# Attention values times weights on TensorE: high and low parts of the values as one stationary operand of 128 columns

## Chip, cores and metric

One NeuronCore of a Trainium2 chip runs the whole program. The metric is the device time of one execution in microseconds (us). The kernel before takes 1706.34 us, the median of 3 runs (1706.33 to 1706.62).

## What is computed

A decoder block on 1024 tokens of 1024 channels, in float32: a root-mean-square norm, one wide input projection, then two mixers side by side (dilated attention and a gated convolution), gates that merge them, an output projection, and a gated feed-forward part. The change concerns the attention. There are three groups of 8 heads of 64 channels, with windows and dilations (128, 1), (512, 4), (2048, 16). A query sees the keys at multiples of the dilation in its window. Cut to what matters:

```python
s = einsum('brnqhd,brnkhd->brnhqk', qb, kb) * Dh ** -0.5 + bias   # scores
s = where(valid, s, -1e30)
lse = logsumexp(s)
p = exp(s - lse)
o = einsum('brnhqk,brnkhd->brnqhd', p, vb)                        # values times weights
...
alpha = softmax(stack(lses), axis=0)       # the groups are merged per head
o = einsum('gbsh,gbshd->bshd', alpha, stack(outs))
```

The kernel keeps nearly float32 accuracy with fp32r matmuls: an operand x is split into a high part `hi`, rounded to fp32r, and a low part `lo = x - hi`, and a product is taken as hi·hi + hi·lo + lo·hi.

## The kernel before

The program is recorded in one fixed order by Python generators (`manual_schedule`), and each engine takes its own instructions in that order. The tile framework adds the semaphores. The order comes from three hand-written devices:

- The main line issues long runs of matmuls (`unit`, `prod`, `v`). After every few of them it calls `tick()`, which moves background generators and steps due at a given tick (`later`), and `beat()`, which moves the attention generator `att` by credit: 0.42 steps per beat while the value projection runs (`RV`), 0.8 afterwards (`RU`).
- `attention` runs 96 steps, one for each pair of heads, group and block of 128 queries (12 passes of 8 blocks), and 5 more to empty its pipeline. Step s issues the scores of block s (`att_s`, L1069 on TensorE, L1072 on VectorE, which adds the bias and takes the row minimum), the exponentials of block s-1 (`att_e`, L1082 on ScalarE), the transposes of the weights of block pair s-4 (`att_t`, L1107 on TensorE; ScalarE copies the high part out of the bank, L1114, VectorE subtracts for the low part, L1115), and the value products of s-5 (`att_p`, L1142). Each `yield` lets matmuls of the main line come between.
- A step k serves one head (k even: first, k odd: second) of a pair of query blocks. So two steps fill one bank, and 48 such pairs of steps make up the stretch.

`att_p` multiplies, for each key block, the values (stationary, keys on the partitions) with the transposed weights (moving, up to 256 queries). The value tile `v` holds, for each key block, 64 columns of high part and then 64 of low part for each head (`value_parts`, L930 on ScalarE, L931 on GpSimd). The three products high·hi, low·hi and high·lo are three matmuls with 66 stationary columns (64 that count and two of what follows) into the same 66 partitions of a bank of tag "o" (2 banks). For the last low part of a tile, which has nothing behind it, GpSimd copies the 64 columns into a small tile `vx` with two zero columns (L935). After the second head VectorE copies the 64 partitions of the bank to the output tile `O`, head by head, 256 queries each, in the order of tokens (L1162). `O` goes to DRAM, and `merge` reads it back for the weighted sum over groups.

The buffers of the stretch: 11 half tiles of 128x512 (tag "c", for scores, hi and lo of the transposed weights, and bias), 42 tiles of 128x1024 (tag "b"), 3 ring tiles (tag "d", among them `O`), and banks g, s, t, o of two each.

Beside the attention run the value projection (L961, L962, with the copy L972 by ScalarE and the sum L983 by GpSimd), then a gate's projection and the convolution's output projection (L318 to L320, weights split in L190/L191), the splits of values' weights (L201/L202) and of the convolution (L1262/L1263), and doubling copies of the queries on GpSimd (L899, L900). SP issues nearly all DMAs, in its own order: loads of queries and keys (L883, L884, L890), bias (L492), values (L911 to L916), convolution (L1333), attention outputs (L1169 out, L1217 back), weights (L177).

Of the kernel before, what the change touches and what calls it, by code (L numbers as in the profile page):

```python
# [10 lines left out]
F32R = mybir.dt.float32r  # L11
AF = mybir.ActivationFunctionType
OP = mybir.AluOpType
# [45 lines left out]
def f(ap):  # L59
    return ap.bitcast(F32)  # L60


class Build:
# [372 lines left out]
    def consts(self):  # L436
        nc = self.nc
        self.ident = self.small.tile([128, 128], F32, name="ident")
        nc.gpsimd.dma_start(self.ident, self.p_ident)
        self.vx = [self.small.tile([128, 66], F32R, name=f"vx{i}") for i in range(4)]  # L440
        for x in self.vx:
            nc.gpsimd.memset(f(x[:, 64:]), 0.0)
        self.mean_col = self.small.tile([128, 1], F32, name="mean_col")
        nc.vector.memset(self.mean_col, 1.0 / D)
        self.eps_rms = self.small.tile([128, 1], F32, name="eps_rms")
        nc.vector.memset(self.eps_rms, RMS_EPS)
        self.eps_ln = self.small.tile([128, 1], F32, name="eps_ln")
        nc.vector.memset(self.eps_ln, LN_EPS)

        warm = self.tiny(1, "warm", 1)  # L450
        nc.scalar.activation(warm, self.eps_ln, AF.Square)
# [473 lines left out]
    def value_parts(self, x, i):  # L925

        v = self.slot(F32R)
        d = v.rearrange("p (t e c) -> p t e c", t=8, e=2)
        y = x[:, i * H:(i + 1) * H].rearrange("p (t c) -> p t c", t=8)
        self.nc.scalar.copy(d[:, :, 0], y)  # L930
        self.nc.gpsimd.tensor_tensor(d[:, :, 1], y, f(d[:, :, 0]), op=OP.subtract)  # L931

        w = self.vx[self.vi % 4]
        self.vi += 1
        self.nc.gpsimd.tensor_copy(w[:, :64], f(d[:, 7, 1]))  # L935
        return v, w

    def v(self, g, hg, now, then):

# [47 lines left out]


    LT, LP = 4, 5
    vi = 0  # L990

    normed = 0

    def attention(self):

        live, s, total = {}, 0, 96
        order = [(g, 2 * hg + i) for hg in range(2) for g in range(3) for i in range(2)]
        nxt, cur, u, x, V = self.stacks(*order.pop(0)), None, 8, None, None
        for i in range(5):
            self.stack_load(nxt)  # L1000
        second, doubled = self.stacks(*order.pop(0)), 0

        def there():
            return nxt[1] // 2 * 3 + nxt[0] < self.vn

        while s < total + self.LP:
            if s < total:
                if x is None and nxt and there():
                    x = self.values(*nxt[:2])
                if u == 8:  # L1010
                    while self.normed < 9 or x is None:
                        if second and second[5] < min(5, self.normed - 6):
                            self.stack_load(second)
                        if cur is None and doubled < min(2, self.normed - 5):
                            self.double(nxt, doubled)
                            doubled += 1
                        if x is None and there():
                            x = self.values(*nxt[:2])
                        yield 0
                    cur, u, nxt, V = nxt, 0, None, []  # L1020
                    self.ending = s == total - 8
                live[s] = a = {}
                self.att_s(a, cur, V, u)
                u += 1

                if u in (4, 5):
                    if len(V) < 2:
                        V.append(self.value_parts(x, u - 4))
                    if u == 5:
                        x = None  # L1030
                if u == 6 and cur[0] == 2:
                    self.other_stats(cur)
                if u in (6, 7) and nxt:
                    self.double(nxt, u - 6)
                if u == 8:
                    cur[2] = cur[3] = V = None
                if u == 1:
                    if second:
                        nxt, second = second, None
                    elif order:  # L1040
                        nxt = self.stacks(*order.pop(0))
                if nxt and nxt[5] < 5:
                    self.stack_load(nxt)
            if 0 <= s - 1 < total:
                self.att_e(live[s - 1])
            yield 0
            if 0 <= s - self.LT < total:
                self.att_t(live, s - self.LT)
                yield 0
            if 0 <= s - self.LP < total:  # L1050
                yield from self.att_p(live, s - self.LP)
            s += 1

    def att_s(self, a, p, V, u):
        nc = self.nc
        g, hp, ops, bt, st = p[:5]
        if g == 0:
            blocks = [u - 1, u] if u else [u]
        elif g == 1:
            blocks = [u - 1, u] if u % 2 else [u]  # L1060
        else:
            blocks = [u]
        n = 128 * len(blocks)
        q, k = slice(u * 128, (u + 1) * 128), slice(blocks[0] * 128, blocks[0] * 128 + n)
        ps = self.bank("s")
        for hh in range(2):
            y, *x = ops[hh]
            for i in range(2):
                nc.tensor.matmul(ps[:, hh * 256:hh * 256 + n], x[i][:, q], y[:, k], start=i == 0, stop=i == 1)  # L1069
        sp = self.half()  # L1070
        for hh in range(2):
            nc.vector.tensor_tensor_reduce(sp[:, hh * 256:hh * 256 + n], ps[:, hh * 256:hh * 256 + n],  # L1072
                                           bt[:, hh * 256 + 256 - n:(hh + 1) * 256], 1.0, 3e38, OP.add, OP.min,
                                           st[:, g, self.place(g, u), hh:hh + 1])
        a.update(g=g, hp=hp, u=u, blocks=blocks, sp=sp, V=V, p=p, n=n)
# [42 lines left out]
    def att_p(self, live, k):  # L1118


        nc = self.nc
        a, b, hh = live[k & ~1], live[k | 1], k & 1
        g, hp, u = a["g"], a["hp"], a["u"]
        if hh == 0:
            a["o"] = self.bank("o")
        ps = a["o"]
        hi, lo = a.pop(("pt", hh))

        if g == 2:
            todo = [(u, 0, 128, 0), (u + 1, 128, 128, 128)]  # L1130
        else:
            n = 256 + 128 * (len(a["blocks"]) > 1)
            todo = [(u, 0, 256, 0)] + [(u - 1, 256, 128, 0)] * (n > 256) + [(u + 1, n, 128, 128)]
        for j, (kb, x, n, q) in enumerate(todo):
            kb = self.place(g, kb)
            v, w = a["V"][kb // 4]
            c = (kb % 4) * 256 + hh * 128
            vh = v[:, c:c + 66]
            vl = v[:, c + 64:c + 130] if c < 896 else w
            o = ps[0:66, hh * 256 + q:hh * 256 + q + n]  # L1140
            for i, (y, z) in enumerate(((vh, hi), (vl, hi), (vh, lo))):
                nc.tensor.matmul(o, y, z[:, x:x + n], start=i == 0 and j == 0, stop=i == 2 and j == len(todo) - 1,  # L1142
                                 skip_group_check=True)
            if j < 2:
                yield 0
        hi = lo = v = w = vh = vl = y = z = None
        if hh == 0:
            return
        if u == 0:
            self.O = self.ring()  # L1150

        O = self.O
        e = (8, 2, 128)[g]
        if g == 0:
            d = O.rearrange("p (c m) -> p m c", c=8)[:, u * 16:u * 16 + 32]
        elif g == 1:
            d = O.rearrange("p (e c m) -> p c m e", e=2, c=4)[:, u // 2]
        else:
            d = O[:, u * 128:u * 128 + 256].rearrange("p (c m) -> p c m", c=2)
        for h in range(2):  # L1160
            x = ps[0:64, h * 256:(h + 1) * 256]
            nc.vector.tensor_copy(d[h * 64:(h + 1) * 64], x.rearrange("p (a e) -> p a e", e=e))  # L1162
        a["o"] = ps = d = x = O = None
        del live[k - 1], live[k]
        if u == 6:

            kept = g == 2 and hp > 1
            if not kept:
                self.later(6, lambda x=self.O: nc.sync.dma_start(self.d_att[g, hp], x))  # L1169
            if g == 2:  # L1170
                self.merges.append(self.bg(self.merge(hp, a["p"][4], self.O if kept else None)))
            self.O = None
# [885 lines left out]
```

## Time and profile before

| | |
|---|---|
| median of 3 runs | 1706.34 us |
| span of the profiled execution, first to last instruction | 1704.7 us |
| TensorE (PE) busy | 1686.8 us, 99% |
| weight loads (PEld) busy | 1417.7 us, 83% |
| VectorE (DVE) busy | 1260.4 us, 74% |
| ScalarE (ACT) busy | 800.6 us, 47% |
| GpSimd (POOL) busy | 499.0 us, 29% |
| granted TensorE clock | 1.000 |
| first and last start of the value products (L1142) | 623.7 and 860.0 us |
| main line from the value projection to L318 | at 792.4 us |
| main line from L318 to the output projection (L1671) | at 969.1 us |

How the profile is read: times are from the start of the span. A row of a group names line, engine, operation, tiles (out<-in, buffer numbers left out), shapes and count; then the time that the group was busy, the mean length of one in ns, and the idle time of its engine just before it with what ended it. A matmul's shape is given as rows*columns of the stationary operand and then the moving operand (128*66 128x256: 66 stationary columns, 256 moving ones). Matmuls overlap each other, so the lengths of single ones add up to more than the time they take, and TensorE's time is read from the distance of their starts. PEld is the loading of stationary operands, which runs beside the matmuls.

### The profile page before, as it was taken

Reading aid. Unit: us, or ns where it says so; the run is one execution under the profiler, and the core shown is the slowest. Engines: PE = TensorE matmul, PEld = TensorE weight load, DVE = VectorE, ACT = ScalarE, POOL = GpSimd, SP = SyncE. Lnnn points to the kernel's source line nnn. Section 1 sums busy time; section 2 is a strip of 40 time slices with the busy share of each in tenths; the row PEclk is TensorE's granted clock in tenths of the full one; section 3 lists DMA queues with packets and bytes.
Section 4 is the critical chain, followed back from the end, with each engine's and each line's share of the span. In section 5 each row is a group of like instructions: output and inputs, shape, how many; then the busy total and the mean of one; then the engine's idle time right before and its main releaser. Section 6 shows DMA issues by size and latency. Waiting matters only on the chain.

```text
span 1704.7 us, 23850 instructions
## 1 busy us (share of the span) xinstructions
PE 1686.8 (99%) x8374; PEld 1417.7 (83%) x8374; DVE 1260.4 (74%) x2216; ACT 800.6 (47%) x1574; POOL 499.0 (29%) x397
## 2 busy tenths in 40 slices
PE   8999999999999999999999999999999999999998
PEld 7788888888888889999888888888888888888886
DVE  6789988888999767777885845675565556677686
ACT  6344344434444576777712436633333333354463
POOL 0017777887886254655300310000000000000000
PEclk9999999999999999999999999999999999999999
DMA  4252433455567887778998722133223322494234
GB/s 166 104 185 87 149 124 130 152 196 177 173 167 176 269 266 211 222 218 224 311 290 294 254 74 88 68 111 112 93 93 112 111 93 93 155 376 137 102 133 155
DMA packets 162357, 283.39 MB, mean 166 GB/s; under 512 B 47249, under 2 KB 78732, under 8 KB 162236
## 3 DMA queue, kind: packets, MB, share of 16 engines
q1 hardware_dynamic: 161516, 281.18, 51.2%
q8 instruction: 66, 1.08, 0.3%
q0 software_dynamic: 432, 0.42, 0.1%
q14 instruction: 55, 0.45, 0.1%
q10 hardware_dynamic: 288, 0.27, 0.0%
HBM read 191.10 MB, written 95.42 MB: 168 GB/s over the span
## 4 chain that ended last, share of the span: by engine, by line
PE 94%; DMA 2%; ACT 1%; POOL 1%; issue 1%; DVE 1%; SPq 0%; DVEq 0%; ACTq 0%; POOLq 0%
PE p L334 15%; PE p L335 15%; PE p L336 15%; PE p L1942 12%; PE p L961 5%; PE p L1671 5%; PE p L318 5%; PE p L320 5%; PE p L319 5%; PE p L1142 3%; PE p L962 2%; PE p L1069 2%; PE p L569 2%; PE p L1107 2%; DMA b<-dk 1%
## 5 line engine op out<-in xcount | busy, mean ns | idle before, releaser
L334 PE MATMUL p<-b,b 128*128 128x512 f32 x1204 | 469.3, 390 | 0.5 <-ACT c L353 0.3
L335 PE MATMUL p<-b,b 128*128 128x512 f32 x1204 | 469.0, 389 | 0.0
L336 PE MATMUL p<-b,b 128*128 128x512 f32 x1204 | 468.9, 389 | 0.0
L334 PEld LDWEIGHTS p<-b,b 128*128 128x128 f32 x1204 | 226.1, 188 | 48.5 <-DVE c L853 1.0
L336 PEld LDWEIGHTS p<-b,b 128*128 128x128 f32 x1204 | 226.0, 188 | 47.0
L335 PEld LDWEIGHTS p<-b,b 128*128 128x128 f32 x1204 | 226.1, 188 | 46.8
L1942 PE MATMUL p<-b,b 128*128 128x512 f32 x924 | 209.6, 389 | 0.0
L1942 PEld LDWEIGHTS p<-b,b 128*128 128x128 f32 x924 | 173.5, 188 | 35.9
L699 DVE SCALAR_TENSOR_TENSOR p<-b,par,p 128x511 f32<-128x511 f32 (+14 forms) x232 | 163.3, 738 | 0.0
L318 PE MATMUL p<-b,b 128*128 128x512 f32 x368 | 147.3, 400 | 0.0
L961 PE MATMUL p<-b,b 128*128 128x512 f32 x384 | 145.0, 410 | 0.0
L320 PE MATMUL p<-b,b 128*128 128x512 f32 x368 | 143.8, 391 | 0.0
L319 PE MATMUL p<-b,b 128*128 128x512 f32 x368 | 143.6, 390 | 0.0
L208 ACT CAST b<-d 128x1024 fp32r<-128x1024 f32 x86 | 90.4, 1051 | 105.2 <-POOL d L229 55.1
L209 POOL TENSOR_TENSOR b<-d,b 128x1024 fp32r<-128x1024 f32 x44 | 106.9, 2430 | 79.9 <-ACT b L208 72.5
L209 DVE TENSOR_TENSOR b<-d,b 128x1024 fp32r<-128x1024 f32 x42 | 51.3, 1221 | 101.0 <-ACT b L208 101.0
L1263 DVE TENSOR_TENSOR b<-b,b 128x512 fp32r<-128x512 f32 x133 | 92.0, 696 | 23.2 <-ACT b L1262 21.2
L962 PE MATMUL p<-b,b 128*128 128x256 f32 x384 | 107.7, 281 | 0.0
L1262 ACT CAST b<-b 128x512 fp32r<-128x512 f32 x133 | 82.1, 619 | 47.6 <-PE p L1942 18.4
L1671 PE MATMUL p<-b,b 128*128 128x512 f32 x384 | 89.4, 392 | 0.0
L1082 ACT ACTIVATE c<-c,stat 128x128 f32<-128x128 f32 (+1 forms) x192 | 85.1, 447 | 6.7 <-DVE stat L1072 6.6
L208 ACT CAST b<-b 128x1024 fp32r<-128x1024 f32 x47 | 49.5, 1052 | 78.7 <-POOL b L236 37.2
(234 smaller groups left out, 2910.5 us busy)
## 6 DMA issues: line engine op xcount, KB each, us to landing
b<-w_in SPq DMA_DIRECT2D x30, 512.0 KB, 4.8
dk<-c SPq DMA_DIRECT2D x48, 256.0 KB, 3.0
dq<-c SPq DMA_DIRECT2D x48, 256.0 KB, 3.6
b<-dq SPq DMA_DIRECT2D x48, 256.0 KB, 3.9
b<-dk SPq DMA_DIRECT2D x48, 256.0 KB, 7.1
b<-w_fi SPq DMA_DIRECT2D x24, 512.0 KB, 4.7
d<-w_in SPq DMA_DIRECT2D x23, 512.0 KB, 4.1
dqS<-c SPq DMA_DIRECT2D x44, 256.0 KB, 2.1
```

What stands on the lines that cost most here:

```text
L209: self.wsplit.tensor_tensor(lo, x, f(hi), op=OP.subtract)
L318: nc.tensor.matmul(ps, hi[:, s], a, start=kt == 0, stop=False)
L319: nc.tensor.matmul(ps, hi[:, s], b, start=False, stop=False)
L320: nc.tensor.matmul(ps, lo[:, s], a, start=False, stop=kt == nk - 1)
L334: nc.tensor.matmul(ps, hi[:, s], a, start=first and kt == 0, stop=False, skip_group_check=True)
L335: nc.tensor.matmul(ps, hi[:, s], b, start=False, stop=False, skip_group_check=True)
L336: nc.tensor.matmul(ps, lo[:, s], a, start=False, stop=kt == 3, skip_group_check=True)
L699: nc.vector.scalar_tensor_tensor(A[i][:, j:], src[i][:, :H - j], w[i], A[i][:, j:], op0=OP.mult, op1=OP.add)
L961: nc.tensor.matmul(ps, a, w, start=kt == 0, stop=kt == KT - 1, skip_group_check=True)
L962: nc.tensor.matmul(ps[:, 256:], b, w[:, :256], start=False, stop=kt == KT - 1, skip_group_check=True)
L1671: nc.tensor.matmul(banks[tt][nh], st, wt[:, nh * H:(nh + 1) * H], start=bool(kt == 0 and a), stop=bool(kt == KT - 1 and b))
L1942: nc.tensor.matmul(acc[t], x, y, start=first and e == 0, stop=last and e == 2, skip_group_check=True)
```

## The change

In `att_p`, high and low part of a head's values, which lie side by side in `v`, become one stationary operand of 128 columns. One matmul with the high part of the weights gives high·hi in the bank's partitions 0 to 63 and low·hi in 64 to 127; a second one, with 66 columns as before, adds high·lo to the lower partitions 0 to 65. When both heads are done, ScalarE copies partitions 64 to 127 of the bank into a half tile `low`, and VectorE adds this to partitions 0 to 63 while it writes `O`, in place of its copy. That add is recorded one step later, behind the next block's scores and exponentials (`self.added`). The small tiles `vx`, their four memsets and their 24 copies go.

```diff
@@ value_parts
-        w = self.vx[self.vi % 4]
-        self.vi += 1
-        self.nc.gpsimd.tensor_copy(w[:, :64], f(d[:, 7, 1]))
-        return v, w
+        return v
@@ attention
             if 0 <= s - 1 < total:
                 self.att_e(live[s - 1])
             yield 0
+            if self.added:
+                self.added()
+                self.added = None
             if 0 <= s - self.LT < total:
                 self.att_t(live, s - self.LT)
                 yield 0
             if 0 <= s - self.LP < total:
                 yield from self.att_p(live, s - self.LP)
             s += 1
+        self.added()
+        self.added = None
@@ att_p
-            vh = v[:, c:c + 66]
-            vl = v[:, c + 64:c + 130] if c < 896 else w
-            o = ps[0:66, hh * 256 + q:hh * 256 + q + n]
-            for i, (y, z) in enumerate(((vh, hi), (vl, hi), (vh, lo))):
-                nc.tensor.matmul(o, y, z[:, x:x + n], start=i == 0 and j == 0, stop=i == 2 and j == len(todo) - 1,
-                                 skip_group_check=True)
+            o = ps[:, hh * 256 + q:hh * 256 + q + n]
+            nc.tensor.matmul(o, v[:, c:c + 128], hi[:, x:x + n], start=j == 0, stop=False, skip_group_check=True)
+            nc.tensor.matmul(o[0:66], v[:, c:c + 66], lo[:, x:x + n], start=False, stop=j == len(todo) - 1,
+                             skip_group_check=True)
             if j < 2:
                 yield 0
         if hh == 0:
             return
+        low = self.half()
+        nc.scalar.copy(low[0:64], ps[64:128])
+        del live[k - 1], live[k]
+        self.added = lambda: self.att_o(a, ps, low)
+
+    def att_o(self, a, ps, low):
...
         for h in range(2):
-            x = ps[0:64, h * 256:(h + 1) * 256]
-            nc.vector.tensor_copy(d[h * 64:(h + 1) * 64], x.rearrange("p (a e) -> p a e", e=e))
+            x, y = (z[0:64, h * 256:(h + 1) * 256].rearrange("p (a e) -> p a e", e=e) for z in (ps, low))
+            nc.vector.tensor_tensor(d[h * 64:(h + 1) * 64], x, y, op=OP.add)
```

The rest of what was the end of `att_p` (the ring tile `O`, its order of tokens, the DMA to DRAM, the start of `merge`) moves into `att_o` unchanged and so also comes one step later.

More of the change, by code (lines that the diff above doesn't have):

```diff
@@ L439, in consts @@
         nc.gpsimd.dma_start(self.ident, self.p_ident)
-        self.vx = [self.small.tile([128, 66], F32R, name=f"vx{i}") for i in range(4)]
-        for x in self.vx:
-            nc.gpsimd.memset(f(x[:, 64:]), 0.0)
         self.mean_col = self.small.tile([128, 1], F32, name="mean_col")
@@ L989 @@
     LT, LP = 4, 5
-    vi = 0
+    added = None
     normed = 0
@@ L1135, in att_p @@
             kb = self.place(g, kb)
-            v, w = a["V"][kb // 4]
+            v = a["V"][kb // 4]
             c = (kb % 4) * 256 + hh * 128
-            vh = v[:, c:c + 66]
-            vl = v[:, c + 64:c + 130] if c < 896 else w
-            o = ps[0:66, hh * 256 + q:hh * 256 + q + n]
-            for i, (y, z) in enumerate(((vh, hi), (vl, hi), (vh, lo))):
-                nc.tensor.matmul(o, y, z[:, x:x + n], start=i == 0 and j == 0, stop=i == 2 and j == len(todo) - 1,
-                                 skip_group_check=True)
+            o = ps[:, hh * 256 + q:hh * 256 + q + n]
+            nc.tensor.matmul(o, v[:, c:c + 128], hi[:, x:x + n], start=j == 0, stop=False, skip_group_check=True)
+            nc.tensor.matmul(o[0:66], v[:, c:c + 66], lo[:, x:x + n], start=False, stop=j == len(todo) - 1,
+                             skip_group_check=True)
             if j < 2:
                 yield 0
-        hi = lo = v = w = vh = vl = y = z = None
+        hi = lo = v = None
         if hh == 0:
             return
+        low = self.half()
[3 more added lines that the diff above has]
+    def att_o(self, a, ps, low):
+        nc = self.nc
+        g, hp, u = a["g"], a["hp"], a["u"]
         if u == 0:
@@ L1160, in att_p @@
         for h in range(2):
-            x = ps[0:64, h * 256:(h + 1) * 256]
-            nc.vector.tensor_copy(d[h * 64:(h + 1) * 64], x.rearrange("p (a e) -> p a e", e=e))
-        a["o"] = ps = d = x = O = None
-        del live[k - 1], live[k]
+            x, y = (z[0:64, h * 256:(h + 1) * 256].rearrange("p (a e) -> p a e", e=e) for z in (ps, low))
+            nc.vector.tensor_tensor(d[h * 64:(h + 1) * 64], x, y, op=OP.add)
+        a["o"] = None
         if u == 6:
```

## The prediction

> **What bounds the kernel now.** I read the page first, for the engine that the end hangs on.
>
> ```profile
> span 1704.7 us, 23850 instructions
> PE 1686.8 (99%) x8374; PEld 1417.7 (83%) x8374; DVE 1260.4 (74%) x2216; ACT 800.6 (47%) x1574; POOL 499.0 (29%) x397
> PE 94%; DMA 2%; ACT 1%; POOL 1%; issue 1%; DVE 1%; SPq 0%; DVEq 0%; ACTq 0%; POOLq 0%
> ```
>
> The median, 1706.34 us, is 1.6 us above this span; I work out a change of the span and apply it to the median. TensorE carries 94% of the chain. The change lies in the attention stretch alone, from the first to the last value product (L1142), so I asked for the engines in windows there.
>
> ```profile
> 617.00:660.00 43.00, 41.16 (x328) 38.33 (x328) 30.57 (x102) 32.78 (x102) 22.25 (x30) 1.00 0.87 246
> ...
> 800.00:831.00 31.00, 31.00 (x225) 27.33 (x225) 27.51 (x85) 25.23 (x83) 18.08 (x25) 1.00 0.91 255
> 831.00:861.00 30.00, 28.71 (x208) 24.42 (x207) 25.03 (x85) 17.90 (x63) 4.96 (x6) 1.00 1.05 300
> sum 244.00, PE 240.88 PEld 221.68 DVE 189.09 ACT 176.61 POOL 120.38; mean PE 48.18 PEld 44.34 DVE 37.82 ACT 35.32 POOL 24.08
> ```
>
> After the window and its length the columns are PE, PEld, DVE, ACT, POOL, granted clock (1.00 all along), DMA share and GB/s. TensorE is idle for 3 us of 244. ScalarE is busy 72% (176.6 of 244), VectorE 77%, and the DMA engines 87% in the first of these windows and 91 and 105% in the last two. So a shorter TensorE stream shortens the stretch, until one of these three sets its length.
>
> **What the matmuls save.** The groups of L1142 by shape, then a few of its matmuls in the timeline (start, length from first start to last end, count):
>
> ```profile
> L1142 PE MATMUL p<-c,b 128*66 128x128 f32 x432 | 48.7, 227 | 0.3 <-DVE c L1115 0.3
> L1142 PE MATMUL p<-c,b 128*66 128x256 f32 x188 | 36.5, 298 | 0.8 <-POOL b L931 0.8
> L1142 PE MATMUL p<-c,vx 128*66 128x128 f32 x24 | 5.4, 223 | 0.0
> L1142 PE MATMUL p<-c,vx 128*66 128x256 f32 x4 | 1.1, 280 | 0.0
> ```
>
> Three matmuls make a product, so there are (432+24)/3 = 152 products over 128 queries and (188+4)/3 = 64 over 256. One matmul of each goes: 216. Matmuls overlap, so what one is worth is not its 227 or 298 ns but the distance between starts:
>
> ```profile
> 720.82 0.34 PE L1142 MATMUL p<-c,b 128*66 128x128 f32 x3
> 721.00 0.61 PE L1069 MATMUL p<-b,b 128*128 128x128 f32 x4
> 721.45 0.41 PE L1107 MATMUL p<-ident,c 128*128 128x128 f32 x2
> ...
> 823.45 0.38 PE L1107 MATMUL p<-ident,c 128*128 128x128 f32 x2
> 823.59 0.36 PE L1142 MATMUL p<-c,b 128*66 128x256 f32 x1
> 823.79 0.28 PE L1142 MATMUL p<-c,vx 128*66 128x256 f32 x1
> 823.91 0.28 PE L1142 MATMUL p<-c,b 128*66 128x256 f32 x1
> 824.02 0.40 PE L318 MATMUL p<-b,b 128*128 128x512 f32 x1
> ```
>
> 128 moving columns against 66 stationary ones: three from 720.82 to 721.00, 0.060 us each. 256 columns: 823.79 to 823.91 to 824.02, 0.115 each. Gross saving 152 x 0.060 + 64 x 0.115 = 9.1 + 7.4 = 16.5 us.
>
> The same rows hold the cost. The scores (L1069) also stream 128 columns, but against 128 stationary columns, and take (721.45 - 721.00)/4 = 0.113 each: loading the wider operand is slower than streaming 128 columns. The new first matmul has 128 stationary columns, so wherever it follows a 128-column matmul it starts 0.113 - 0.060 = 0.053 later than now. In the changed program's order 34 new first matmuls stand directly behind the short second one of the product before: 34 x 0.053 = 1.8 us. 59 more stand behind a transpose. There the rows from 823.45 help: two transposes and the product matmul behind them take 823.79 - 823.45 = 0.34, which is 0.115 for the matmul and 0.113 for each transpose. A transpose already takes as long as the wide load, which then hides beside it, and I count nothing; if it hides nothing it is 59 x 0.053 = 3.1. The other 123 stand behind 256 or 512 columns, which take at least 0.115 and cover the load. TensorE's stream gets shorter by 16.5 - 1.8 = **14.7 us**, bounds 11.6 (all 93 places pay) and 16.5 (none does).
>
> A rule of the Trainium skill speaks against the change here: "TensorE: Matmul & The Clock Gate", section "LDWEIGHTS (loading the stationary operand)", gives a load as columns/1.2 ns, 107 for 128 columns and 55 for 66 as an estimate. The trace agrees (0.113 against 0.060). Taken for all 93 places, transposes included, it makes the saving 11.6.
>
> **What is added on ScalarE and VectorE.** 48 copies of 64x512 out of the bank. No row has that shape; the nearest are L972 (128x512 out of a bank, 585) and the first of L1114.
>
> ```profile
> L972 ACT COPY b<-p 128x512 f32<-128x512 f32 x28 | 16.4, 585 | 0.2 <-PE p L962 0.2
> L1114 ACT CAST c<-p 128x384 fp32r<-128x384 f32 (+2 forms) x96 | 44.9, 468 | 53.3 <-PE p L1107 52.6 <-ACT c L1082 0.3
> L1162 DVE COPY d<-p 64x256 f32<-64x256 f32 x96 | 52.6, 548 | 6.8 <-PE p L1142 5.6
> L1115 DVE TENSOR_TENSOR c<-p,c 128x256 fp32r<-128x256 f32 x32 | 13.4, 420 | 6.6 <-ACT c L1114 6.3
> ```
>
> I take 0.585: 48 x 0.585 = 28.1 us; bounds 48 x 0.3 = 14 (if half the partitions halved it) and 28.1; with 14 the 5 us that I give back below would be some 3. ScalarE then has 204.7 us in a stretch of 244 - 14.7 = 229: 89%. Its present idle is mostly the 52.6 us before L1114, waiting for transposes; the copies eat half of that.
>
> VectorE's 96 copies (mean 548) become 96 adds. An add from a bank over 256 elements costs 420 (L1115), inside the copies' own range, so I count 0; at 420 each it would be 12 us less of VectorE, with 0.1 more each 10 us more, 82% busy becoming 87%. POOL loses 24 small casts; it is idle half of the stretch (120.38 of 244 busy) and TensorE's waits for it are under 1 us (0.8 in the second row of L1142), so nothing. Four memsets at the start go, beside loads. SP's order changes in two places, where merges start one step later (four L1333 loads pass L1208, one L1217 passes L1169): I count nothing, since TensorE's one DMA wait in the stretch (the last row of this part) is for another load; were one of these late, it would cost about what that wait does.
>
> **What the new wait holds up.** The copy waits for the last value product of a pair. Queued behind it on ScalarE are two exponentials (L1082) and the next step's L1114; VectorE's L1115 waits for that, and the next value product for L1115. The adds, now a step later, stand behind two L1072, which wait for that step's scores. One pair of now:
>
> ```profile
> 757.45 0.34 PE L1142 MATMUL p<-c,b 128*66 128x128 f32 x3
> ...
> 757.82 1.25 DVE L1162 COPY d<-p 64x256 f32<-64x256 f32 x2 [0.16 <-PE p L1142]
> 757.86 0.50 ACT L1082 ACTIVATE c<-c,stat 128x256 f32<-128x256 f32 x1
> ...
> 758.84 0.59 ACT L1114 CAST c<-p 128x512 fp32r<-128x512 f32 x1 [0.39 <-PE p L1107]
> ...
> 759.80 0.69 DVE L1115 TENSOR_TENSOR c<-p,c 128x512 fp32r<-128x512 f32 x1
> ...
> 761.49 0.59 PE L1142 MATMUL p<-c,b 128*66 128x256 f32 x3
> ```
>
> The product ends at 757.79. The copy would run to 758.41, two exponentials of 0.50 to 759.4, L1114 to 760.0 instead of 759.43: 0.6 late. The rest of the lower part L1115 follows to 760.7 instead of 760.49, or a little more behind the adds. It is needed at the second matmul, 761.6, and 0.3 earlier still when each of 48 pairs is 14.7/48 shorter. So this pair keeps 0.6 us. The cover is gone where the margin is now under 0.9, as it is from 800 to 831, where VectorE has 27.5 of 31 us and ScalarE 25.2 plus 3.5 for six copies, 28.7 of 30. A pair there, in which L1115 ends 0.4 before its product:
>
> ```profile
> 828.00 0.41 DVE L1115 TENSOR_TENSOR c<-p,c 128x256 fp32r<-128x256 f32 x1
> ...
> 828.75 0.53 PE L1142 MATMUL p<-c,b 128*66 128x128 f32 x6
> ```
>
> Estimate: the 12 pairs of 800 to 861 and two or three elsewhere, 0.3 to 0.4 us each (0.9 less some 0.5), 5 us. The end of the stretch leans on DMA already:
>
> ```profile
> 833.04 0.51 PE L1069 MATMUL p<-b,b 128*128 128x128 f32 x2 [1.02 <-DMA b<-dk]
> ```
>
> With the DMA engines full (1.05) that load will not come earlier by what TensorE gains in the same window; I add 1 us. Sum: -14.7 + 5 + 1 = -8.7. **1706.3 - 8.7 = 1697.6 us**, for this case 1694 to 1702.
>
> **Rivals.**
> - *All of it arrives.* Every margin holds, and ScalarE keeps up at 89% as it does at 81% from 800 to 831 now. 1706.3 - 14.7 = 1691.6, at the bound of 16.5 1689.8. Against it: the stretch 800 to 831.
> - *The wide load costs after transposes too* (then 93 x 0.053 = 4.9 instead of 1.8): saving 11.6, with the same 6 given back 1700.7; the change would do less of what it says. For it: the scores pay that price. Against it: the 0.34 from 823.45. [...]
> - *ScalarE and VectorE set the pace and give all of it back.* Light pairs keep their 0.3; pairs with one more piece in the queue (0.585 from an L972, say) lose it again: in the mean 0.3 a pair, the 14.7 is spent. 1703 to 1709, middle 1706. For it: 204.7 of 229 us on an engine that serves in order.
> - *Slower.* Copy, exponentials, L1114, L1115 and value products become one loop. By the rows: 0.6 + 1.0 + 0.6 + 0.7, hand-overs 0.2, products and the work between them 757.79 - 756.08 = 1.7, together 4.8, against a pair of 244/48 = 5.1 now; one more piece of 0.6 to 0.7 inside makes it 5.4 to 5.5. Where more than half of the pairs hold one, the gain of 0.3 in the rest is used up; with 36 of 48 it is 36 x 0.35 - 12 x 0.3 = +9.0: 1715.3. The row for the pair's first product:
>
> ```profile
> 756.08 0.66 PE L1142 MATMUL p<-c,b 128*66 128x256 f32 x4
> ```
>
> **How the numbers follow.** Chances: forecast 0.50, all of it 0.17, wide load 0.08, given back 0.15, slower 0.10. Predicted is the likeliest, 1697.6. Left out of the range are the slower case and the upper half of the given-back one (0.17); it reaches down to the bound of the full gain: 1690 to 1706. A difference under 0.2% (3.4 us) can hardly be told from none here; faster by more than that are the first three, 0.75; within it 0.15; slower 0.10.
>
> **What would show it.** Right: 432 product matmuls, 0.06 apart or 0.115, with 0.113 only at the 34 places; the stretch 7 to 10 us shorter and the rest as it was; ScalarE near 205 us in it, the copy near 0.59; new idle before product matmuls that ends with L1115 or L1114, a few us in all, most after 800. Wrong: the copy well under 0.5, or no new idle (full gain); transposes followed by a product 0.05 later (wide load); an idle before most products (given back or slower); a gain before 861 that is lost after it, in the loads for the merges; any difference outside the stretch.

## The result, and the profile after

The changed kernel takes 1699.02 us (median of 5 runs, 1697.04 to 1700.21) against 1706.62 us of the kernel before beside it: ratio 0.995, 95% interval 0.9938 to 0.9962. It is 7.6 us faster; 8.7 was forecast, and 1697.6 lies 1.4 us below the measured time. The profiled execution took 1700.21 us, with a span of 1698.4.

Line numbers after: L1067 scores, L1070 reduction, L1080 exponentials, L1105 transposes, L1112 high part and L1113 low part of the weights, L1137 the new matmul of 128 stationary columns, L1138 the second one with 66, L1146 ScalarE's copy, L1167 the adds. First the page: span, engines, chain.

```profile
span 1698.4 us, 23450 instructions
PE 1675.6 (99%) x8158; PEld 1404.2 (83%) x8158; DVE 1256.8 (74%) x2216; ACT 826.8 (49%) x1622; POOL 492.6 (29%) x369
PE 90%; DMA 4%; DVE 2%; ACT 1%; issue 1%; POOL 1%; SPq 0%; DVEq 0%; ACTq 0%; POOLq 0%
```

216 matmuls are gone, TensorE's busy time is 11.2 us less, ScalarE's 26.2 more, VectorE's 3.6 less. The stretch itself is read from two rows of the timeline, the first scores and the last value product. First of before, then of after:

```profile
614.31 0.85 PE L1069 MATMUL p<-b,b 128*128 128x128 f32 x6
...
860.00 0.22 PE L1142 MATMUL p<-c,b 128*66 128x128 f32 x1
```

```profile
616.10 0.96 PE L1067 MATMUL p<-b,b 128*128 128x128 f32 x7
...
853.68 0.23 PE L1138 MATMUL p<-c,b 128*66 128x128 f32 x1
```

From start of the first to end of the last it took 245.9 us and takes 237.8: **8.1 us less**. In this profile it begins 1.8 us later; in a second profile of the same changed kernel (E12 below) it begins at 614.93 and lasts 237.7. In these two profiles the stretch repeats within 0.2 us and the time ahead of it does not, so below I compare kernels by their stretch as well as by their medians. The stretch of each kernel is that of one profiled execution, though, and in three of them (E2, E3, E7) it also holds times at a lower clock, told further down. The windows of after, columns as in the prediction:

```profile
...
800.00:831.00 31.00, 27.60 (x181) 23.53 (x181) 27.33 (x88) 26.33 (x83) 10.58 (x13) 1.00 1.03 308
...
sum 237.00, PE 228.34 PEld 207.86 DVE 186.45 ACT 203.13 POOL 114.27; mean PE 45.67 PEld 41.57 DVE 37.29 ACT 40.63 POOL 22.85
```

From 800 to 831 us TensorE was busy all 31 us before; now it stands idle for 3.4. What it waits for, in total, times and longest, from 617 to 870 us, before and then after:

```profile
PE p L1069 <- DVE stat L1072: 2.3, 2, 1.3
PE p L1069 <- DMA b<-dk: 1.0, 1, 1.0
PE p L1142 <- POOL b L931: 0.8, 1, 0.8
PE p L1142 <- DVE c L1115: 0.3, 1, 0.3
```

```profile
PE p L1138 <- DVE c L1113: 4.9, 7, 1.1
PE p L1067 <- DVE stat L1070: 2.0, 2, 1.0
PE p L1137 <- ACT c L1112: 0.8, 1, 0.8
PE p L1067 <- DMA b<-dk: 0.6, 1, 0.6
```

One wait has grown: that of the second matmul for the lower part of the weights, 0.3 to 4.9 us, of which 4.6 fall after 800 us. By passes (8 steps each, one group and two heads), read off the starts of the scores, the first ten passes shrink from 198.47 to 187.32 us and the last two grow from 47.46 to 50.48. So 11.15 us are gained up to 803 us, and 3.02 are lost behind it. One of the stalls, in the order of time:

```profile
816.63 0.58 ACT L1146 COPY c<-p 64x512 f32<-64x512 f32 x1
...
817.89 0.61 ACT L190 CAST b<-b 128x512 fp32r<-128x512 f32 x1
...
818.53 0.88 DVE L191 TENSOR_TENSOR b<-b,b 128x512 fp32r<-128x512 f32 x1 [0.72 <-ACT b L190]
...
819.33 1.23 DVE L1167 TENSOR_TENSOR d<-p,c 64x256 f32<-64x256 f32 x2
...
820.10 0.35 ACT L1112 CAST c<-p 128x256 fp32r<-128x256 f32 x1
...
820.59 0.42 DVE L1113 TENSOR_TENSOR c<-p,c 128x256 fp32r<-128x256 f32 x1
...
821.07 0.28 PE L1138 MATMUL p<-c,b 128*66 128x128 f32 x1 [1.03 <-DVE c L1113]
```

The copy pushes ScalarE's exponentials and its split of another projection's weights (L190) back; VectorE idles 0.72 us for that split, subtracts, adds twice, and only then makes the lower part that TensorE has been waiting for. A first reading is that the adds cost because they stand ahead of L1113; E2 and E3 test it.

### The profile page after: what moved, and what is told of

Read it like the earlier page. It is cut to its first block, busy times and chain, and to the rows that moved or that the text cites. A ratio compares the mean times of both kernels' runs of the same rounds, so it can differ in the third digit from the quotient of the medians.

```text
span 1698.4 us, 23450 instructions
## 1 busy us (share of the span) xinstructions
PE 1675.6 (99%) x8158; PEld 1404.2 (83%) x8158; DVE 1256.8 (74%) x2216; ACT 826.8 (49%) x1622; POOL 492.6 (29%) x369
## 4 chain that ended last, share of the span: by engine, by line
PE 90%; DMA 4%; DVE 2%; ACT 1%; issue 1%; POOL 1%; SPq 0%; DVEq 0%; ACTq 0%; POOLq 0%
PE p L334 15%; PE p L335 15%; PE p L336 15%; PE p L1946 12%; PE p L1675 5%; PE p L954 5%; PE p L318 5%; PE p L319 5%; PE p L320 5%; PE p L955 2%; PE p L1067 2%; PE p L1105 1%; DMA b<-dq 1%; PE p L1138 1%; PE p L1137 1%
## 5 line engine op out<-in xcount | busy, mean ns | idle before, releaser
L1267 DVE TENSOR_TENSOR b<-b,b 128x512 fp32r<-128x512 f32 x133 | 91.9, 695 | 25.0 <-ACT b L1266 23.2
L1266 ACT CAST b<-b 128x512 fp32r<-128x512 f32 x133 | 82.1, 619 | 47.7 <-PE p L1946 18.4
L1080 ACT ACTIVATE c<-c,stat 128x128 f32<-128x128 f32 (+1 forms) x192 | 85.0, 446 | 0.2 <-DVE stat L1070 0.2
```

## Experiments

All 12 runs, each timed in rounds with the kernel before on the same chip. The stretch is that of each one's profile, first score to last value product.

| kernel | median us | before beside it | ratio, 95% interval | stretch us |
|---|---|---|---|---|
| before | | 1706.62 | | 245.9 |
| changed | 1699.02 | 1706.62 | 0.9950 (0.9938 to 0.9962) | 237.8 |
| E1 TensorE's part alone | 1693.31 | 1706.92 | 0.9917 (0.9904 to 0.9930) | 233.9 |
| E2 adds behind L1113 | 1700.71 | 1706.92 | 0.9957 (0.9945 to 0.9968) | 239.0 |
| E3 copy and adds behind | 1700.37 | 1706.92 | 0.9961 (0.9947 to 0.9975) | 243.7 |
| E4 before, wide loads | 1715.50 | 1706.92 | 1.0048 (1.0036 to 1.0061) | 254.5 |
| E5 E1 and ScalarE's copy | 1698.23 | 1707.80 | 0.9946 (0.9934 to 0.9959) | 236.7 |
| E6 E1, VectorE one step later | 1695.52 | 1707.80 | 0.9934 (0.9921 to 0.9947) | 233.2 |
| E7 changed, copy twice | 1710.25 | 1707.80 | 1.0014 (1.0005 to 1.0023) | 249.7 |
| E8 changed, splits on GpSimd | 1697.03 | 1707.80 | 0.9937 (0.9925 to 0.9950) | 235.0 |
| E9 E5, copy from other data | 1696.79 | 1707.27 | 0.9937 (0.9922 to 0.9953) | 235.1 |
| E10 E8, value casts on GpSimd | 1695.84 | 1707.27 | 0.9929 (0.9914 to 0.9944) | 232.4 |
| E11 before, splits on GpSimd | 1708.21 | 1707.27 | 1.0004 (0.9995 to 1.0012) | 246.6 |
| E12 the changed kernel again | 1698.29 | 1707.27 | 0.9945 (0.9930 to 0.9960) | 237.7 |

### E1: TensorE's part alone

```diff
-            if self.added:
-                self.added()
-                self.added = None
...
-        low = self.half()
-        nc.scalar.copy(low[0:64], ps[64:128])
+        low = None
         del live[k - 1], live[k]
-        self.added = lambda: self.att_o(a, ps, low)
+        self.att_o(a, ps, low)
...
-            nc.vector.tensor_tensor(d[h * 64:(h + 1) * 64], x, y, op=OP.add)
+            x = ps[0:64, h * 256:(h + 1) * 256]
+            nc.vector.tensor_copy(d[h * 64:(h + 1) * 64], x.rearrange("p (a e) -> p a e", e=e))
```

The kernel leaves the product of the values' low part out of its result, as E5, E6 and E9 do.

> Of the change only TensorE's part: two matmuls in place of three, 128 columns stationary. ScalarE copies nothing, and VectorE copies the bank's lower half at the place and time that the kernel before has (left out: the product of the values' low part). Theory (TensorE saves 14.7 us, of which the copy, the adds and their order give some 5 to 7 back): about 14.7 below before, 1691 to 1693, and no TensorE wait over 0.5 us for L1113 after 800 us. Rival, wide load paid behind transposes too: 11.6 below, about 1695. Rival, TensorE itself saves only what the change shows and the copy costs nothing: 1698 to 1700, as the changed kernel.

1693.31 us, 13.6 below before, a little above the 1691 to 1693 that was expected; the stretch is 12.1 shorter. This is what arrives of TensorE's saving when ScalarE and VectorE have nothing new to do, against 14.7 forecast. Its waits in the stretch (here L1133 is the second matmul, L1108 the lower part):

```profile
...
PE p L1133 <- DVE c L1108: 1.4, 4, 0.4
PE p L1062 <- DMA b<-dk: 1.2, 1, 1.2
...
```

Even without copy or adds, 1.1 us more are spent on the lower part than before: the shorter TensorE stream alone runs into VectorE, and the last two passes gain nothing (47.7 us against 47.5).

### E2 and E3: the order of the new pieces

E2 records the adds behind the next step's L1113; E3 also moves ScalarE's copy there, behind the exponentials and the high part.

```diff
-            if self.added:
-                self.added()
-                self.added = None
             if 0 <= s - self.LT < total:
                 self.att_t(live, s - self.LT)
+            if self.added:
+                self.added()
+                self.added = None
+            if 0 <= s - self.LT < total:
                 yield 0
```

> The changed kernel with one difference in order: VectorE's two adds stand behind the next step's lower parts (L1113) and not ahead of them. Theory, that 1.2 us of adds ahead of the lower part make the stalls of TensorE after 800 us (some 6 us above those of before): most of them go, 3 to 6 us below the changed kernel, 1693 to 1696. Rival, that the late piece is ScalarE's (the copy ahead of the exponentials and of the high part, for which VectorE waits): under 1.5 us below it, 1697.5 to 1699. Rival, that the bank is held longer and the next products or scores wait for it: slower than the changed kernel, with TensorE waits that end with the add.

> The changed kernel with ScalarE's copy and VectorE's adds both one step later, behind the exponentials and the splits of the next step into high and low part. Theory: nothing of the path from score to product stands behind the new work any more, so nearly all of TensorE's saving arrives, 1691 to 1694, and at most 1.5 us above the kernel that has TensorE's part alone. Rival, that it is ScalarE's and VectorE's total load and not the order: 1696 to 1699, as the changed kernel. Rival, the output bank held a step longer makes the next pair wait: above 1699, with waits for the copy.

1700.71 and 1700.37 us: neither order helps, and the expectations of 1693 to 1696 and 1691 to 1694 fell. In E2 the stalls move (the passes from 724 to 766 us take 41.5 us against 39.5 in the changed kernel, the last two 49.8 against 50.5); TensorE's wait for the lower part is 4.4 us instead of 4.9. So the adds ahead of L1113 are not what costs. E3 is less clear. Its wait for the lower part is 3.2 us, but two of 1.2 and 0.4 us before the first of the two matmuls are new (the longer one ends right behind ScalarE's late high part), and its first ten passes take 188.8 us against 187.3. In neither kernel does a wait of TensorE end with a copy or an add, so the bank that is held longer is not seen to cost. Its profile is of the slowest of its six executions (1704.55 us; the fastest took 1697.93), and the 243.7 us of its stretch hold a wait of 3.2 us for a DMA and two times at half the clock, told under what was not expected. By the medians, and by the fastest execution of each (1697.93 against 1697.04), the order brought nothing; what E3's stretch would be without these accidents stays open.

### E4: the price of a wide load

```diff
-            vh = v[:, c:c + 66]
+            vh = v[:, c:c + 128]
...
-            o = ps[0:66, hh * 256 + q:hh * 256 + q + n]
+            o = ps[:, hh * 256 + q:hh * 256 + q + n]
...
-                nc.tensor.matmul(o, y, z[:, x:x + n], ...
+                nc.tensor.matmul(o if y is vh else o[0:66], y, z[:, x:x + n], ...
```

> The kernel before, its three matmuls kept; the high part of the values is 128 columns wide as a stationary operand in two of the three (the upper half of the bank that this fills is not read). So only weight loads get longer: of 128 columns in place of 66. By the estimate of 0.053 us for each such load directly behind a matmul of 128 columns (152 inside the products, 34 at the first of a group): 9.9 us slower, 1716. If a load behind a transpose pays too (59 more): 13.0, 1719. If a load's width costs nothing: 1706, and TensorE's saving in the changed kernel would then be the full 16.5.

8.6 us, by the medians and by the stretch. The nearest expectation is 9.9, a price behind 128-column matmuls only; 13.0 is out, and so is nothing. Over 186 places it is 0.046 us each instead of 0.053; TensorE's waits fell at the same time (that for the keys' load from 1.0 to 0.3, that for L1115 from 0.3 to none), which makes up most of the difference. That transposes cover the load is seen in the changed kernel directly. Two products of 128 queries, the first behind two transposes, the second directly behind the first:

```profile
711.53 0.38 PE L1105 MATMUL p<-ident,c 128*128 128x128 f32 x2
711.66 0.31 PE L1137 MATMUL p<-c,b 128*128 128x128 f32 x1
711.81 0.22 PE L1138 MATMUL p<-c,b 128*66 128x128 f32 x1
711.86 0.28 PE L1137 MATMUL p<-c,b 128*128 128x128 f32 x1
711.98 0.23 PE L1138 MATMUL p<-c,b 128*66 128x128 f32 x1
```

From the transposes to the second L1137 it is 0.33 us, where 2 x 0.113 and 2 x 0.06 make 0.35: nothing is left for the wide load of the first L1137. Behind the second one the next start comes 0.12 later, twice the 0.05 to 0.06 of an L1138. By the medians of all such places (start of the matmul ahead of the product to start of what follows the product), a product of 128 queries got shorter by 0.059 us behind transposes (0.292 to 0.233, 19 places), by 0.058 behind 256 columns (0.296 to 0.238, 83), and by 0.009 directly behind another short one (0.244 to 0.235, 34); one of 256 queries by 0.115 (0.462 to 0.347 behind transposes, 40).

### E5, E6, E7: ScalarE or VectorE

E5 is E1 plus ScalarE's copy, which nobody reads. E6 is E1 with VectorE's two pieces one step later, as in the changed kernel. E7 is the changed kernel with the copy made twice.

```diff
 E5, against E1
-        low = None
+        low = self.half()
+        nc.scalar.copy(low[0:64], ps[64:128])
 E6, against the changed kernel
-        low = self.half()
-        nc.scalar.copy(low[0:64], ps[64:128])
+        low = None
...
-            nc.vector.tensor_tensor(d[h * 64:(h + 1) * 64], x, y, op=OP.add)
+            x = ps[0:64, h * 256:(h + 1) * 256]
+            nc.vector.tensor_copy(d[h * 64:(h + 1) * 64], x.rearrange("p (a e) -> p a e", e=e))
 E7, against the changed kernel
         nc.scalar.copy(low[0:64], ps[64:128])
+        nc.scalar.copy(low[0:64], ps[64:128])
```

> TensorE's part alone, as in the kernel that came out at 1693.3, and with it ScalarE's 48 copies of 64x512 into a buffer that nobody reads; VectorE copies the lower half at once (left out, as there: the low part's product). So ScalarE carries the load of the change and VectorE's work and order stay those of before. Theory now, after the two orders changed nothing: it is ScalarE's load of 28 us (it is 86 to 88% busy then) that gives most of it back, 1697 to 1699. Rival, the adds one step later on VectorE, standing ahead of other work there: 1693 to 1694.5, as without the copy.

> The other half: no copy on ScalarE, but VectorE's two pieces (plain copies of the lower half, the low part's product left out) stand one step later, where the changed kernel has its adds. ScalarE's load as before. Theory, ScalarE's load: 1693 to 1694.5, nothing given back. Rival, VectorE's order: 1697 to 1699. If both halves cost, each some 2 to 3 us: 1695 to 1696.5 here and in the run with the unread copy.

> The changed kernel with ScalarE's copy made twice into the same buffer, so 28 us more on ScalarE from 617 to 854 us, 98% of that time. Theory, ScalarE's load: the stretch becomes ScalarE's and 6 to 15 us are lost against the changed kernel, 1705 to 1714, above before or near it, with TensorE waits for L1112 and L1113 in all of the stretch. Rival, the copy is hidden and something else gives the time back: under 2 us, 1699 to 1701.

Most of it is ScalarE's. Its copies alone bring E1 from 1693.31 to 1698.23 us (ratio 0.9917 to 0.9946, stretch 233.9 to 236.7), nearly the changed kernel's time, though nobody reads them. VectorE's pieces one step later add nothing to the stretch: E6's is 0.6 shorter than E1's. Its median, 1695.52 us, lies in the 1695 to 1696.5 that was noted for the case that both halves cost, and not in the 1693 to 1694.5 of the theory; its ratio's interval overlaps E1's and E5's both, so the medians alone do not separate the halves. TensorE's wait for the lower part, in E5 and then in E6, against 1.4 us in E1:

```profile
PE p L1133 <- DVE c L1108: 2.9, 8, 0.8
```

```profile
PE p L1138 <- DVE c L1113: 2.5, 4, 1.1
```

In E6 it grew by 1.1 us, while the 1.2 us for the keys' load are not there; so the late position may cost a little that this profile hides. The last 1.1 us of stretch from E5 to the changed kernel, which has both halves, no run divides.

The second copy costs 11.9 us of stretch, where the first cost at most 4: E7 is 2.4 us slower than before. Its window over the stretch, and the waits:

```profile
617.00:866.00 249.00, 236.23 (x1669) 211.42 (x1670) 187.41 (x633) 228.49 (x673) 113.92 (x135) 0.99 0.83 238
```

```profile
PE p L1138 <- DVE c L1113: 7.8, 12, 1.7
...
```

ScalarE is busy 228.5 of 249 us there, 92%, and now the first ten passes pay too (195.8 us against 187.3), at the full clock. The last two take 3.5 us more than in the changed kernel, and there the clock fell twice to half for 3.4 us, which accounts for up to 3.4 of them. At 72% of load, before, 28 us more on it took 3 to 5 us of time; at 86%, the same 28 took some 8 to 12, depending on whether the clock's share is counted.

### E8 to E12: room on ScalarE

E8 moves the 16 splits of the next stage's input (L1266 on ScalarE and L1267 on VectorE, 786 to 847 us) to GpSimd, so it makes room on both engines; E10 also the 24 high parts of the values (L927), which are ScalarE's alone; E11 makes E8's move in the kernel before; E12 is the changed kernel once more. E9 is E5 with the copy reading a tile of values instead of the bank.

```diff
 E8
-        nc.scalar.copy(s[:, :n], src)
-        nc.vector.tensor_tensor(s[:, 512:512 + n], src, f(s[:, :n]), op=OP.subtract)
+        e = nc.gpsimd if pool else nc.vector
+        (nc.gpsimd.tensor_copy if pool else nc.scalar.copy)(s[:, :n], src)
+        e.tensor_tensor(s[:, 512:512 + n], src, f(s[:, :n]), op=OP.subtract)
...
-            self.cop[i // 8].append(self.split(x[0][:, i % 2 * H:(i % 2 + 1) * H], H))
+            self.cop[i // 8].append(self.split(x[0][:, i % 2 * H:(i % 2 + 1) * H], H, True))
 E10, besides
-        self.nc.scalar.copy(d[:, :, 0], y)
+        self.nc.gpsimd.tensor_copy(d[:, :, 0], y)
 E9, against E5
-        nc.scalar.copy(low[0:64], ps[64:128])
+        nc.scalar.copy(low[0:64], f(a["V"][0][64:128, 0:512]))
```

> The changed kernel, and the 16 splits of the next stage's input (L1266 on ScalarE, 0.62 us, and L1267 on VectorE, 0.73 us, from 786 to 847 us) go to GpSimd, which is nearly idle from 800 us on (13.7 of 61 us). Takes 9.9 us off ScalarE and 11.7 off VectorE, where TensorE stalls most. Theory, load of the two engines after 800 us: 2 to 5 us below the changed kernel, 1694 to 1697, with waits for L1113 after 800 us down from 4.6 to under 2 us. Rival, the DMA engines, full after 800 us, set the end (one load of keys is waited for): no gain, 1698 to 1700, and the waits for the keys grow instead. Rival, GpSimd's splits (two pieces of some 1.3 us each) are late for their own products after 854 us: slower than the changed kernel.

> As the run with the unread copy, but ScalarE's 48 copies of 64x512 read a tile of values that was there long before, so that they wait for nothing (TensorE's part of the change stands, the low part's product is left out, VectorE copies at once). Theory, ScalarE's load: as the unread copy with its wait, 1696.5 to 1699, some 3 to 5 above TensorE's part alone. Rival, the wait of the copy for the end of the products, with two exponentials and the high part queued behind it, is what costs: 1693 to 1694.5.

> The kernel with the next stage's splits on GpSimd, and there also the high parts of the values (L927, 24 casts of 0.62 us), so that ScalarE carries 24.8 us less than in the changed kernel and only 3 more than before. Theory, ScalarE's load: what is left between that kernel and TensorE's part alone (235.0 against 233.85 us of the stretch) goes as well, 1693 to 1696, the stretch 233.5 to 234.5. Rival, GpSimd, 62% busy in the stretch then and over 80% from 800 us on, is late with the values' low parts: TensorE waits for L928 and 1698 or more.

> The kernel before with the next stage's splits on GpSimd and nothing else. If that move pays only because it makes room for the change's copies and adds: within 1 us of before, 1706 to 1707.5 (before waits 1.6 us in all after 800 us, 1.0 of it for a DMA). If it is a gain of its own: 2 us below before or more.

> The changed kernel itself, on the same chip as the three beside it, so that a microsecond or two between them can be told: 1698 to 1700.5 and a stretch of 237 to 239 us; each theory expects the same here.

E8 takes 2.8 us off the stretch, all of it after 783 us (the wait for L1113 falls from 4.9 to 1.3 us in all); its median, 1697.03, just misses the 1694 to 1697 expected. E10 takes 5.3 off: 232.4 us, 1.5 less than E1 and below the 233.5 to 234.5 expected, with the copies and the adds in it. Its waits, and its busy times over the stretch:

```profile
...
PE p L1067 <- DMA b<-dk: 0.8, 1, 0.8
PE p L319 <- POOL b L1268: 0.7, 1, 0.7
...
PE p L1138 <- DVE c L1113: 0.5, 2, 0.3
...
```

```profile
sum 230.00, PE 226.32 PEld 207.34 DVE 179.90 ACT 182.48 POOL 158.65; mean PE 56.58 PEld 51.83 DVE 44.97 ACT 45.62 POOL 39.66
```

The wait that had grown to 4.9 us is back at 0.5. ScalarE has 79%, VectorE 78, GpSimd 69 (62 was expected). In the kernel before E8's move is worth nothing (E11, interval 0.9995 to 1.0012; its median is 0.9 us above before's), so in the changed kernel it pays for what the change put there. E10's further move was not tried in the kernel before, and some 0.9 us of its gain may come there too: the wait before the first value product, at 624 us, which the kernel before has as its 0.8 us for L931, is gone in E10. E10 is the fastest of the runs that leave nothing out, 1695.84 us against 1698.29 of the changed kernel on the same chip and 1707.27 before; by these runs alone the two intervals overlap, by the stretch it is ahead by 5.3 us. Why only 2.5 of these show in the medians stays open; executions of one kernel differ by more than that (1694.44 to 1697.89 us for E10).

E9 should have told the wait of the copy from its work. Its median, 1696.79 us, lies in the range for ScalarE's load (1696.5 to 1699); by its stretch it came out between: 1.5 us less than E5, 1.3 more than E1. The row of the copy, E5 first, then E9, shows that it still waited, 6.0 us in all, as I read it for a free half tile (L1132 and L1133 are the products, the last readers of one):

```profile
L1141 ACT COPY c<-p 64x512 f32<-64x512 f32 x48 | 28.0, 584 | 10.9 <-PE p L1133 9.8
```

```profile
L1141 ACT COPY c<-b 64x512 f32<-64x512 f32 x48 | 29.7, 619 | 6.0 <-PE p L1132 3.5 <-PE p L1133 1.1 <-POOL d L976 0.4
```

So how much of the copy's price is its wait for the products and how much its 0.58 us stays open.

## Why the prediction was right, step by step

**TensorE's saving, -14.7.** Right. By the distances of starts above it is 118 x 0.058 + 34 x 0.009 + 64 x 0.115 = 14.5. The wide load is paid at the 34 places and hidden behind transposes, as counted; E4 costs 8.6 us, not 13.0. The rival of a wide load behind transposes is out. The rule of the Trainium skill ("TensorE: Matmul & The Clock Gate", "LDWEIGHTS (loading the stationary operand)"), 107 ns for 128 columns, is close to the 0.112 us from start to start where such loads set the pace, but as a price it holds only where what is ahead streams for less time than that. (The profile's rows show a single load as 188 ns with 128 columns and 138 with 66; the difference, 50 ns, fits the rule too.)

**ScalarE's copy, 0.585.** Right: 583 ns in the row below. Half the partitions do not halve it. ScalarE has 203.1 us of 237, forecast 204.7 of 229.

```profile
L1167 DVE TENSOR_TENSOR d<-p,c 64x256 f32<-64x256 f32 x96 | 52.8, 550 | 3.2 <-ACT c L1146 2.5
...
L1146 ACT COPY c<-p 64x512 f32<-64x512 f32 x48 | 28.0, 583 | 13.2 <-PE p L1138 11.8 <-ACT c L1112 0.4
```

**VectorE's adds, 0.** Right for their length: 52.8 us and 550 ns each, the copies had 52.6 and 548. The late position lengthens no stretch by itself (E6), though the wait for the lower part grows by 1.1 us there.

**What the new wait gives back, +5.** Right in size and place, partly by another way than the text gave. All distances between starts that exceed a matmul's own by over 0.18 us add up to some 5.5 us in the stretch of before, 11.8 after, 8.4 in E1 and 6.7 in E10. So about 6.3 are given back, and 14.5 - 6.3 = 8.2 is near the 8.1 of the stretch. About 3 of the 6.3 are there in E1, without any copy: they are the margin that the shorter pairs use up, which the text had as "0.3 earlier still". The other 3.4 come with the copies and adds; E5 shows 2.8 us of stretch for the copies alone. Nor do the stalls spread over 14 pairs at 0.3 to 0.4 each: six of 0.6 to 1.3 us between 809 and 848 us hold about 6 us. In the one shown a late piece on ScalarE makes one on VectorE late and with it the next. That 14 x 0.35 came to the right size is in part luck.

**The keys' load, +1.** Not so: its wait went from 1.0 to 0.6 us in the changed kernel. It rose to 1.2 in E1 and 3.2 in E3. It moves with the run of the last passes and was no fixed term; that 5 + 1 meets the 6.3 so well is luck too.

**GpSimd and SP, 0.** Nothing in the waits speaks against it.

**The rivals.** That all arrives would need the copy to be free; E1 shows that not even TensorE's part arrives whole, and E10 comes within 1.0 us of it (13.5 of 14.5). That ScalarE sets the pace and gives all back, and the loop that ends slower than before, are both there one copy further on: E7, at 92% of ScalarE, 1710.25 us, of which the falls of the clock are a part.

## What to carry to other kernels

Price a matmul by the distance of starts and a wider stationary operand by what streams ahead of it: the load costs only what the moving columns ahead of it don't cover. When work is put on an engine that is off the path but 70 to 80% busy beside a full TensorE, its price is not nothing and not its length: here 28 us cost some 4, and the next 28 cost 8 to 12. Look first for other work of that engine that an idle third one can take; moving the new work about in the order brought nothing here.

## What was not expected of the hardware

**The clock after stalls.** In E3 one load of keys came 3.19 us late, and TensorE ran slower afterwards. Timeline, and granted clock in windows (columns: window, its length, PE busy, clock, DMA share, GB/s):

```profile
822.77 0.39 PE L1068 MATMUL p<-b,b 128*128 128x128 f32 x2
826.35 0.66 PE L1068 MATMUL p<-b,b 128*128 128x128 f32 x2 [3.19 <-DMA b<-dk]
...
827.34 0.63 PE L319 MATMUL p<-b,b 128*128 128x512 f32 x1
827.77 0.63 PE L320 MATMUL p<-b,b 128*128 128x512 f32 x1
```

```profile
822.77:824.90 2.13, 0.38 (x5) 1.00 1.03 276
824.90:826.35 1.45, 0.00 (x1) 0.50 1.03 388
826.35:831.70 5.35, 5.35 (x21) 0.50 1.00 351
```

The clock is at half from 824.90 on, 1.75 us into the stall and not at its end. A matmul of 512 columns then takes 0.43 us from start to start (827.34 to 827.77) instead of 0.23, until 831.6. No such long wait is needed. In E2 (where L1139 is the second matmul and L1114 the lower part) two stalls of 0.81 and 1.11 us, close together, were enough, and the clock was at half from 848.5 to 851.9:

```profile
846.31 0.30 PE L1138 MATMUL p<-c,b 128*128 128x128 f32 x1 [0.81 <-issue]
847.72 0.27 PE L1139 MATMUL p<-c,b 128*66 128x128 f32 x1 [1.11 <-DVE c L1114]
```

```profile
848.00:850.00 2.00, 2.00 (x9) 0.61 1.02 252
850.00:852.00 2.00, 2.00 (x9) 0.53 1.02 225
```

In E7 a single stall of 1.69 us was enough. The first window ends where the clock falls, the second where it rises again:

```profile
830.45 0.27 PE L1138 MATMUL p<-c,b 128*66 128x128 f32 x1 [1.69 <-DVE c L1113]
```

```profile
828.17:831.58 3.41, 1.72 (x13) 1.00 1.04 333
831.58:834.99 3.41, 3.41 (x15) 0.50 1.06 397
```

So a stall can cost more than itself: in E2 about 1.7 us more (4 us at a clock of 0.57). The Trainium skill, in "TensorE: Matmul & The Clock Gate", "Part 1: The HAM clock gate", has the clock fall after an idle window of about 3.4 us. These traces show it after windows that were only about half idle: in the 3.41 us before each of the five falls in the stretches of E2, E3 and E7, TensorE stood idle for 1.6 to 2.1 us in all. That is near the limit here: E4, with 1.64 us idle from 620.11 to 623.52, kept its clock. The changed kernel's own stalls, of which the longest by its waits is 1.1 us, left the clock at 1.00.

**Partitions and memories.** ScalarE's copy of 512 columns takes as long for 64 partitions out of a bank (584 ns) as for 128 (587, L965), and a little longer out of SBUF (619). GpSimd casts a 128x512 tile in 610 ns (L927 in E10), no slower than ScalarE (622), while its subtraction of that size takes 1337.
